# A two-layer decoder trunk: the branch products get PSUM banks of their own, the first merged chunk is split alone, and three steps move later

## The chip, the cores and the metric

The kernel runs on one core of a Trainium2 chip. The metric is the device time of one execution in microseconds (us); lower is better. The engines are called by the names of the profile: PE (TensorE) multiplies matrices, PEld loads its stationary operand, DVE and ACT work element by element, POOL is the fourth engine, and SP issues most of the transfers (DMA).

## The reference

The program computes two layers on x of 256 tokens by 1024 columns, in float32. Cut to what matters here, a layer's first half is:

```python
proj = x @ w_in                      # q, k, v of 8 heads, twice, and two gates of 1024
o_sb = stick_breaking_attention(...) # 256 x 512
o_mb = moba_attention(rope(q_mb), rope(k_mb), v_mb)   # here: causal softmax attention, 256 x 512
merged = sigmoid(g_sb) * (o_sb @ w_branch_sb) + sigmoid(g_moba) * (o_mb @ w_branch_moba)
x = layer_norm(ALPHA * x + merged @ w_out)
```

The second half of a layer is a SwiGLU block with its own normalization, which the change doesn't touch.

## The kernel before, in words

**Arithmetic.** Every float32 operand of a product is held as two parts: `hi`, the value cast to fp32r on ACT, and `lo`, the rest, which DVE subtracts. A product is three matmuls, hi·hi, hi·lo and lo·hi (`mm3`, L433). `split_line` (L349) makes the two parts. Weights come in 122 granules of 128 x 1024 values for each layer. SP loads a granule into one of 6 `raw` buffers, ACT casts it to `whi`, and DVE subtracts to `wlo` (`WeightStream.line`, L159). The next load into a raw buffer waits for the `wlo` of the granule that had it. Both rings hold 10 granules, and `ws.allow` frees a place when PE is done with it.

**Order.** All instructions are recorded by one Python program, in the order in which they will stand on their engines. `Weave` (L35) keeps a planned clock for each engine. Side work is written as generators ("lines") that yield the planned time from which they may go on; while the main program records matmuls, `weave.tick` records every line whose time has come, and `weave.finish` records lines to their end. So a number that is yielded moves instructions on their engines' queues, and every engine works its queue strictly in order.

**PSUM.** There are eight banks, in three pools. `bankM` (L297) gives two tiles of one bank in turn, `bankC` two of one bank, `bankB` two tiles of two banks. An instruction waits for the earlier users of the tile that it writes, and the waits are kept by tile: a matmul into the second bank of a `bankB` tile waits for a DVE read of its first bank.

**Stage by stage.** First come the projections: v and q (`pv`, `pq`), the stick-breaking pairs (`pqk`), k of the second attention (`pk`), its v (`pu`), then eight gate chunks (`pg`, L867), 48 matmuls of 256 columns each. Two heads make a pair, and four pairs of each attention go beside those matmuls. k of the second attention is turned by a round trip through DRAM (`bounce_line`, L511), and `put_kmb` (L884) splits it into `l0kmb_hi` and `l0kmb_lo`. The weights of a pair of the second attention are turned the same way and split into `pp`. Then four matmuls (`l0mb_o`) make the weighted sums of a pair, in two tiles: `bankC` for pairs 0 to 2, `bankM` for pair 3 (`both_parts`, L627). ACT copies one half of each to `f`, DVE adds the rest (four instructions named `l0mb_f`), and `split_line` makes `l0omb_hi` and `l0omb_lo`.

**Around the change.** `branch(i, b, ...)` (L914) multiplies chunk pair i (256 of the 1024 columns) of branch b: 24 matmuls of 256 columns into one bank, over four pairs k of heads. Branch 0 (`l0pa`) needs the first attention and goes while the last pairs of the second one are under way; branch 1 (`l0pb`) needs pair k of the second attention for its k-th part. Before, pa of i = 0 and 1 are the two banks of one `bankB` tile, and so are i = 2 and 3; the same holds for pb. After a branch DVE multiplies its bank with the sigmoid of the gate (`l0gate<-l0gate,l0pa`), for branch 1 it adds the two (`l0gate<-l0gate`), and `split_line` makes the merged chunk pair `l0m_hi`, `l0m_lo`. Branch 1 is recorded as the k = 0, 1 and the k = 2 part of i = 0 to 2, then for each i what is left: 6, 6, 6 and 24 matmuls. Last, `l0pw` multiplies the merged chunks c = 0 to 7 with w_out, for tokens 0 to 127 and then for the rest, in matmuls of 512 columns, six for each chunk; the lo part of a chunk is first used by its third matmul. Layer 1 is the same, with names that begin with l1.

Of the kernel before, what the change touches and what calls it, by code (L numbers as in the profile page):

```python
# [14 lines left out]
P = 128  # L15
DEPTH = 2
D = 1024
S = 256
KC = D // P
DH = 64  # L20
WIDTH = 512
NPAIR = 4
# [12 lines left out]
class Weave:  # L35
# [16 lines left out]
    def dve(self, e, n, f, *args, **kw):  # L52
        f(*args, **kw)  # L53
        self.dve_t = max(self.dve_t, e) + n / 960.0 + DVE_FIXED
        return self.dve_t + HOP
# [195 lines left out]
NSPLIT = 10  # L251
# [9 lines left out]
MARGIN = 0.29  # L261
# [7 lines left out]
def hybrid_trunk_kernel(ctx: ExitStack, tc: tile.TileContext, w, xT_in, x_in, ln_in,  # L269
                        ident_in, mask_in, rope_in, out):  # L270
    nc = tc.nc
# [25 lines left out]
    def bankM(name, shape):  # L297
        return psM.tile(shape, F32, tag="M", name=name)
# [26 lines left out]
    ws = WeightStream(nc, wpool, rings, w, DEPTH * NG_LAYER, weave)  # L325
    act, dve, pool = weave.act, weave.dve, weave.pool
# [72 lines left out]
    hi, lo = (part[:, first[0]] for part in ws.parts[0])  # L399
    e = dve(3.6, 512, nc.vector.tensor_copy, hi, ws.raw[0][:, first[0]])  # L400
# [14 lines left out]
    def late_loads():  # L415
        nc.sync.dma_start(ident, ident_in)
        nc.sync.dma_start(rope, rope_in)
        nc.sync.dma_start(mask, mask_in)
        yield 118.0
        for t in range(2):  # L420
            nc.sync.dma_start(xs[t], x_in[t * P:(t + 1) * P, :])

    weave.add(late_loads(), 12.0)


# [17 lines left out]
    def pe_after(e):  # L443
        weave.t = max(weave.t, e)

    def pe_done():
        return weave.t + HOP
# [80 lines left out]
    def blocked(x):  # L528
        return x.rearrange("p n (i b) -> p n i b", b=32)
# [94 lines left out]
        e = yield from split_line(*parts, pT, 768, e)  # L624
        yield from both_parts(name, p, v, oT, e, p == NPAIR - 1)

    def both_parts(name, p, v, oT, e, in_M=False):  # L627

        turns = []
        if in_M:
            os = [bankM(f"{name}_o{h}", [P, 2, S]) for h in range(2)]
        else:
            for h in range(2):
                turns.append((yield from turn(e)))
            os = [bankC(f"{name}_o{h}", [P, 2, S]) for h in range(2)]
        pe_after(e)
        for h, o in enumerate(os):
            vs = [x[:, p, 2 * h:2 * h + 2, :].rearrange("p r c -> p (r c)") for x in v]  # L640
            mm(o, vs[0], pp[:, :, h, :S], True, False)
            mm(o[:, :, P:], vs[1], pp[:, :, h, S:], False, True)
        e = pe_done()
        summed.append(e)
        yield e
        f = page2.tile([P, S], F32, tag="f", name=f"{name}_f")
        for h, o in enumerate(os):
            e = act(e, S, nc.scalar.copy, f[ROWS[h]], o[ROWS[1 - h], 0, :])
        yield e
        for h, o in enumerate(os):  # L650
            for i in range(2):
                e = dve(e, S, nc.vector.tensor_add, f[ROWS[h]], o[ROWS[h], i, :], f[ROWS[h]])
            if not in_M:
                left[turns[h]] = e
        yield e
        yield from split_line(oT[0][:, p, :], oT[1][:, p, :], f, S, e)
# [150 lines left out]
    for l in range(DEPTH):  # L807
        G = l * NG_LAYER
        L = f"l{l}"
# [18 lines left out]
        else:  # L828
            for t in range(2):
                weave.finish(norms[:t + 1])  # L830
                pe_after(xT_ready[t])
                for j, put in enumerate((put_v, put_q)):
                    ps = bankM(f"{L}pvq{j}{t}", [P, WIDTH])
                    for i in range(4):
                        g = G + 4 * j + i
# [9 lines left out]
        sides, sigmoids, exps, gates, waiting = [], [], [], [], []  # L845
# [36 lines left out]
        k_mb = pair_tiles(L + "kmb", [P, NPAIR, S])  # L882

        def put_kmb(tp, ts, e):  # L884
            return split_line(*(blocked(k[:, :, ts]) for k in k_mb), tp, WIDTH, e)

        both_tokens(f"{L}pk", G + 12, lambda t, ps: ropes.append(weave.start(rope_line(L + "kmb", ps, t, put_kmb))))
        sb_pair(2, G + 16)
# [20 lines left out]
        def rooted():  # L909
            for dst in waiting:  # L910
                act(0.0, 512, nc.scalar.activation, dst, dst, AF.Sigmoid)
            waiting.clear()

        def branch(i, b, ps, ks=range(4)):  # L914
            g = G + 40 + 4 * b + i
            hi, lo = (x.rearrange("p (c k n) -> p c k n", c=2, k=4) for x in ws.take(g))
            o = (o_sb, o_mb)[b]
            for c in range(2):
                for k in ks:
                    mm3(ps[:, c, :], hi[:, c, k, :], lo[:, c, k, :], o[0][:, k, :], o[1][:, k, :],  # L920
                        c == k == 0, c == 1 and k == 3)
            if ks[-1] < 3:
                return 0.0
            ws.allow(g + NSPLIT)
            gated = gates[i][:, :, b, :]
            return dve(pe_done(), 512, nc.vector.tensor_mul, gated, gated, ps)

        if len(exps) == NPAIR:
            rooted()
        for i in range(4):  # L930
            if i % 2 == 0:
                ps = bankB(f"{L}pa{i}", [P, 2, 2, S])
            branch(i, 0, ps[:, i % 2])
        weave.finish(sides[:mb])
        weave.finish(sides[:-2])
        rooted()


        gb = load_gb(l, 0)
        m_t = [pair_tiles(f"{L}m{i}", [P, 4, S]) for i in range(2)]  # L940

        def m_parts(c, n=1):
            return [m[:, c % 4:c % 4 + n, :] if n > 1 else m[:, c % 4, :] for m in m_t[c // 4]]

        pbs = [x for i in range(2) for x in bankB(f"{L}pb{i}", [P, 2, 2, S]).rearrange("p i c n -> i p c n")]
        for ks, upto in ((range(2), -1), (range(2, 3), None)):
            for i in range(3):
                branch(i, 1, pbs[i], ks)
            weave.finish(sides[:upto])
        for i in range(4):  # L950
            e = branch(i, 1, pbs[i], range(3 if i < 3 else 0, 4))
            a, b = (gates[i][:, :, j, :] for j in range(2))
            e = dve(e, 512, nc.vector.tensor_add, a, a, b)
            weave.add(split_line(*m_parts(2 * i, 2), a, 512, e), e)


        norms = []
        for t in range(2):
            acc = bankB(f"{L}pw{t}", [P, 2, 512])
            for c in range(KC):  # L960
                token_out([(512 * h, acc[:, h, :]) for h in range(2)], G + 48 + c, t, *m_parts(c), c == 0, c == KC - 1)
                if t == 1:
                    ws.allow(G + 48 + NSPLIT + c)
            norms.append(weave.start(norm_line(f"{L}a", t, acc, gb)))
# [29 lines left out]
        sides = []  # L994
        for t in range(2):
            weave.finish(norms[:t + 1])
            pe_after(xT_ready[t])
            for j in range(2):
                ps = bankM(f"{L}pft{t}{j}", [P, 512])
                for i in range(4):  # L1000
                    g = G + 56 + 4 * j + i
# [4 lines left out]
        for c in range(NTOK_FC, NFC):  # L1006
            ps = bankM(f"{L}pf{c}", [P, 2, S])
# [12 lines left out]
        g = G + 100  # L1020
# [102 lines left out]
```

## Time and profile before

| | us |
|---|---|
| median of 3 runs (734.68 to 735.06) | 734.88 |
| the profiled execution | 734.4 |
| its span, from the first to the last instruction | 732.5 |
| PE busy, of the span | 712.8 |
| DVE busy | 529.2 |
| ACT busy | 389.1 |
| mean granted clock of TensorE, as a share of full speed | 0.997 |

The profile lists instructions with start and duration in us from the start of the span, the engine, L and the line of the program (helpers have one line: L427 is every matmul, L53 every DVE and L48 every ACT instruction), the operation, and what it writes and reads by the program's names. In brackets stands how long the engine was idle before the instruction and which instruction ended the wait. "x4" is four instructions in a row. Matmuls overlap: one of 256 columns has 0.28 us from start to end, and the next starts 0.11 us after it.

### The profile page before, as it was taken

The numbers are of one execution on the slowest core, as the hardware profiler recorded it, in microseconds if no ns is written. First come the engines' busy times: TensorE is split into PE (matmuls) and PEld (weight loads), VectorE is DVE, ScalarE is ACT, GpSimd is POOL, SyncE is SP. The second block draws the span as 40 slices with busy tenths as digits, with TensorE's granted clock in tenths as the row PEclk, the third lists the DMA queues.
The fourth block names the chain that finished last, engine by engine and source line by source line (L and its number), as shares of the span: only waits on it lengthen the run. The fifth ranks groups of instructions, "written<-read, shape, count | busy, mean of one in ns | idle before, by whom it ended". The sixth has DMA issues, their size and how long they took to land.

```text
span 732.5 us, 12710 instructions
## 1 busy us (share of the span) xinstructions
PE 712.8 (97%) x4984; PEld 652.8 (89%) x4984; DVE 529.2 (72%) x784; ACT 389.1 (53%) x579; POOL 34.5 (5%) x48
## 2 busy tenths in 40 slices
PE   9999999889999999999999999998899999999995
PEld 7989899878899999988889889998788999998885
DVE  5998887688896666644688886868879766665416
ACT  5767667564565554533365566774456545554400
POOL 0001110000000000000000111100010000000001
PEclk9999999999999999999999999999999999999998
DMA  8898889847696656476259678795558965663601
GB/s 301 328 343 222 250 215 268 261 135 238 192 322 227 198 196 198 147 286 200 70 184 342 171 206 232 210 293 193 160 186 263 314 200 199 185 198 104 235 1 58
DMA packets 61597, 156.26 MB, mean 213 GB/s; under 512 B 10721, under 2 KB 21985, under 8 KB 61537
## 3 DMA queue, kind: packets, MB, share of 16 engines
q1 hardware_dynamic: 56848, 140.50, 57.0%
q0 software_dynamic: 4544, 14.68, 9.3%
q8 instruction: 39, 0.64, 0.4%
q10 hardware_dynamic: 144, 0.26, 0.1%
q14 instruction: 22, 0.17, 0.1%
HBM read 148.08 MB, written 7.34 MB: 212 GB/s over the span
## 4 chain that ended last, share of the span: by engine, by line
PE 92%; DVE 4%; DMA 2%; issue 1%; ACT 0%; POOL 0%; DVEq 0%; POOLq 0%; SPq 0%; ACTq 0%
PE l1pf L427 13%; PE l0pf L427 13%; PE l0pd L427 8%; PE l0pg L427 6%; PE l1pg L427 6%; PE l1pe L427 4%; PE l1pd L427 4%; PE l1pft L427 3%; PE l0pw L427 3%; PE l1pqk L427 3%; PE l0pft L427 3%; PE l1pvq L427 3%; PE l1pw L427 3%; PE l0pqk L427 2%; PE l0pv L427 2%; PE l1pk L427 2%
## 5 line engine op out<-in xcount | busy, mean ns | idle before, releaser
L53 DVE TENSOR_TENSOR wlo<-raw,whi 128x1024 fp32r<-128x1024 f32 (+1 forms) x234 | 277.5, 1202 | 82.8 <-ACT whi L48 79.5
L48 ACT CAST whi<-raw 128x1024 fp32r<-128x1024 f32 (+1 forms) x233 | 238.0, 1035 | 84.4 <-PE l0pd L427 19.6
L427 PE MATMUL l1pf<-xT_hi,wlo 128*128 128x256 f32 x288 | 79.6, 276 | 0.0
L427 PE MATMUL l1pf<-xT_hi,whi 128*128 128x256 f32 x288 | 79.6, 276 | 0.0
L427 PE MATMUL l1pf<-xT_lo,whi 128*128 128x256 f32 x288 | 79.6, 276 | 0.0
L427 PE MATMUL l0pf<-xT_hi,wlo 128*128 128x256 f32 x288 | 79.5, 276 | 0.0
L427 PE MATMUL l0pf<-xT_hi,whi 128*128 128x256 f32 x288 | 79.5, 276 | 0.0
L427 PE MATMUL l0pf<-xT_lo,whi 128*128 128x256 f32 x288 | 79.5, 276 | 0.0
L427 PEld LDWEIGHTS l1pf<-xT_hi,whi 128*128 128x128 f32 x288 | 54.1, 188 | 0.0
L427 PEld LDWEIGHTS l1pf<-xT_lo,whi 128*128 128x128 f32 x288 | 54.1, 188 | 0.0
L427 PEld LDWEIGHTS l1pf<-xT_hi,wlo 128*128 128x128 f32 x288 | 54.1, 188 | 0.0
L427 PEld LDWEIGHTS l0pf<-xT_lo,whi 128*128 128x128 f32 x288 | 54.1, 188 | 0.0
L427 PEld LDWEIGHTS l0pf<-xT_hi,whi 128*128 128x128 f32 x288 | 54.1, 188 | 0.0
L427 PEld LDWEIGHTS l0pf<-xT_hi,wlo 128*128 128x128 f32 x288 | 54.1, 188 | 0.0
L427 PE MATMUL l0pg<-xT_hi,whi 128*128 128x256 f32 x128 | 35.8, 280 | 0.8 <-DVE l0vmb L53 0.8
L427 PE MATMUL l1pg<-xT_hi,whi 128*128 128x256 f32 x128 | 35.7, 279 | 0.0
L427 PE MATMUL l0pg<-xT_hi,wlo 128*128 128x256 f32 x128 | 35.4, 277 | 0.0
L427 PE MATMUL l0pg<-xT_lo,whi 128*128 128x256 f32 x128 | 35.4, 277 | 0.0
L427 PE MATMUL l1pg<-xT_hi,wlo 128*128 128x256 f32 x128 | 35.4, 276 | 0.0
L427 PE MATMUL l1pg<-xT_lo,whi 128*128 128x256 f32 x128 | 35.4, 276 | 0.0
L427 PE MATMUL l0pd<-whi,l0h_hi 128*128 128x512 f32 x88 | 34.5, 392 | 0.0
L427 PE MATMUL l0pd<-whi,l0h_lo 128*128 128x512 f32 x88 | 34.3, 389 | 0.0
(349 smaller groups left out, 1784.6 us busy)
## 6 DMA issues: line engine op xcount, KB each, us to landing
raw<-in_w_dram SPq DMA_DIRECT2D x226, 512.0 KB, 4.7
whi<-in_w_dram POOLq DMA_DIRECT2D x14, 512.0 KB, 5.8
wlo<-in_w_dram POOLq DMA_DIRECT2D x14, 512.0 KB, 6.7
ln<-in_ln_dram SPq DMA_DIRECT2D x8, 512.0 KB, 4.2
raw<-in_w_dram SPq DMA_DIRECT2D x7, 256.0 KB, 5.2
l0mb_scr<-l0mb_turn SPq DMA_DIRECT2D x4, 384.0 KB, 4.9
l0mb_turn<-l0mb_scr SPq DMA_DIRECT2D x16, 96.0 KB, 5.3
l1mb_scr<-l1mb_turn SPq DMA_DIRECT2D x4, 384.0 KB, 8.0
```

The source lines that it names most:

```text
L48: f(*args, **kw)
L53: f(*args, **kw)
L427: nc.tensor.matmul(o, a, b, start=start, stop=stop)
```

## The change

- **pa**: each i has a `bankM` tile of one bank, the two tiles in turn, and its gate multiply is recorded right behind its matmuls.
- **pb**: i = 0 and 1 have a `bankM` tile each; i = 2 and 3 share one `bankB` tile, and both of their gate multiplies come after the last matmul of i = 3. The k = 0, 1 part of i = 3 moves ahead of the end of pair 3, so that 12 instead of 24 matmuls are left for it.
- **Last pair**: the weighted sums of pair 3 go to one `bankB` tile, and the line yields `e + MARGIN` ahead of it, so it is recorded later.
- **First chunk**: of the merged pair i = 0 the two chunks are multiplied, added and split one by one, 256 columns each; i = 1 to 3 stay whole. The splits of i = 0 are finished only after the matmuls of i = 3 are recorded, and the others as `l0pw` comes to them.
- **k cast**: `put_kmb` yields `e + 4.0` first.
- **Late loads**: the loads of x are planned at 130 instead of 118, and the scale and shift of the norm (`load_gb`) are recorded after the last pair instead of before it.

```diff
-        yield 118.0
+        yield 130.0
         for t in range(2):
             nc.sync.dma_start(xs[t], x_in[t * P:(t + 1) * P, :])
...
-    def both_parts(name, p, v, oT, e, in_M=False):
+    def both_parts(name, p, v, oT, e, in_B=False):
         turns = []
-        if in_M:
-            os = [bankM(f"{name}_o{h}", [P, 2, S]) for h in range(2)]
+        if in_B:
+            yield e + MARGIN
+            both = bankB(f"{name}_o", [P, 2, 2, S])
+            os = [both[:, h] for h in range(2)]
...
         def put_kmb(tp, ts, e):
-            return split_line(*(blocked(k[:, :, ts]) for k in k_mb), tp, WIDTH, e)
+            yield e + 4.0
+            yield from split_line(*(blocked(k[:, :, ts]) for k in k_mb), tp, WIDTH, e)
...
-            gated = gates[i][:, :, b, :]
-            return dve(pe_done(), 512, nc.vector.tensor_mul, gated, gated, ps)
-        if len(exps) == NPAIR:
-            rooted()
+        def gated(i, b, ps, cs=slice(0, 2)):
+            dst = gates[i][:, cs, b, :]
+            return dve(pe_done(), ps.shape[1] * S, nc.vector.tensor_mul, dst, dst, ps)
+        rooted()
         for i in range(4):
-            if i % 2 == 0:
-                ps = bankB(f"{L}pa{i}", [P, 2, 2, S])
-            branch(i, 0, ps[:, i % 2])
+            ps = bankM(f"{L}pa{i}", [P, 2, S])
+            branch(i, 0, ps)
+            gated(i, 0, ps)
         weave.finish(sides[:mb])
         weave.finish(sides[:-2])
-        rooted()
+        pbs = [bankM(f"{L}pb{i}", [P, 2, S]) for i in range(2)]
+        ps = bankB(f"{L}pb2", [P, 2, 2, S])
+        pbs += [ps[:, 0], ps[:, 1]]
+        for i in range(3):
+            branch(i, 1, pbs[i], range(2))
+        weave.finish(sides[:-1])
+        for i in range(3):
+            branch(i, 1, pbs[i], range(2, 3))
+        branch(3, 1, pbs[3], range(2))
+        weave.finish(sides)
+        pe_after(weave.dve_t)
         gb = load_gb(l, 0)
...
-        pbs = [x for i in range(2) for x in bankB(f"{L}pb{i}", [P, 2, 2, S]).rearrange("p i c n -> i p c n")]
-        for ks, upto in ((range(2), -1), (range(2, 3), None)):
-            for i in range(3):
-                branch(i, 1, pbs[i], ks)
-            weave.finish(sides[:upto])
+        def summed_up(i, c0, n):
+            cs = slice(c0, c0 + n)
+            gated(i, 1, pbs[i][:, cs], cs)
+            a, b = (gates[i][:, cs, j, :] for j in range(2))
+            e = dve(0.0, n * S, nc.vector.tensor_add, a, a, b)
+            hi, lo = (m[:, (2 * i + c0) % 4:(2 * i + c0) % 4 + n, :] for m in m_t[i // 2])
+            side = weave.add(split_line(hi, lo, a, n * S, e), e)
+            m_sides.extend([side] * n)
+        m_sides = []
         for i in range(4):
-            e = branch(i, 1, pbs[i], range(3 if i < 3 else 0, 4))
-            a, b = (gates[i][:, :, j, :] for j in range(2))
-            e = dve(e, 512, nc.vector.tensor_add, a, a, b)
-            weave.add(split_line(*m_parts(2 * i, 2), a, 512, e), e)
+            branch(i, 1, pbs[i], range(3 if i < 3 else 2, 4))
+            for part in (((0, 0, 1), (0, 1, 1)), ((1, 0, 2),), (), ((2, 0, 2), (3, 0, 2)))[i]:
+                if i == 3:
+                    weave.finish(m_sides[:2])
+                summed_up(*part)
...
             for c in range(KC):
+                weave.finish(m_sides[c:c + 1])
                 token_out(...)
```

What this does to the queues shows at three places. The first is PE in layer 0, where the matmuls of pa pass from i = 0 to i = 1. The number behind a name is its buffer, and in brackets stand the engines whose signal the instruction waits for. Before:

```order
L427 MATMUL l0pa_1609<-l0osb_hi,wlo 128x256
L427 MATMUL l0pa_1609<-l0osb_hi,whi 128x256 [waits DVE_49]
L427 MATMUL l0pa_1609<-l0osb_lo,whi 128x256
L427 MATMUL l0pa_1609<-l0osb_hi,wlo 128x256
L427 MATMUL l0pa_1609<-l0osb_hi,whi 128x256
```

And after, at the same place of the queue:

```order
L427 MATMUL l0pa_1607<-l0osb_hi,wlo 128x256
L427 MATMUL l0pa_1644<-l0osb_hi,whi 128x256 [waits Activation_49]
L427 MATMUL l0pa_1644<-l0osb_lo,whi 128x256
L427 MATMUL l0pa_1644<-l0osb_hi,wlo 128x256
L427 MATMUL l0pa_1644<-l0osb_hi,whi 128x256
```

The tile changes there now, and the wait for DVE's gate multiply has become one for ACT, which read the bank's former user, a gate chunk.

The second place is DVE in layer 0 at the end of the branches, from the gate multiply of i = 0 (gate buffers 935, 1131, 1306 and 1455 are i = 0 to 3; `raw` is a weight granule). Before:

```order
L53 TENSOR_TENSOR l0gate_935<-l0gate_935,l0pb_1766 128x2x256
L53 TENSOR_TENSOR l0gate_935<-l0gate_935 128x2x256
L53 TENSOR_TENSOR l0gate_1131<-l0gate_1131,l0pb_1766 128x2x256
L53 TENSOR_TENSOR l0gate_1131<-l0gate_1131 128x2x256
L53 TENSOR_TENSOR l0gate_1306<-l0gate_1306,l0pb_1767 128x2x256
L53 TENSOR_TENSOR l0gate_1306<-l0gate_1306 128x2x256
L53 TENSOR_TENSOR l0m_lo<-l0gate_935,l0m_hi 128x512
L53 TENSOR_TENSOR l0gate_1455<-l0gate_1455,l0pb_1767 128x2x256
L53 TENSOR_TENSOR l0gate_1455<-l0gate_1455 128x2x256
L53 TENSOR_TENSOR wlo<-raw_1666,whi 128x1024
L53 TENSOR_TENSOR l0m_lo<-l0gate_1131,l0m_hi 128x512
```

After, with gate buffers 931, 1129, 1310 and 1455:

```order
L53 TENSOR_TENSOR l0gate_931<-l0gate_931,l0pb_1754 128x256
L53 TENSOR_TENSOR l0gate_931<-l0gate_931 128x256
L53 TENSOR_TENSOR l0gate_931<-l0gate_931,l0pb_1754 128x256
L53 TENSOR_TENSOR l0gate_931<-l0gate_931 128x256
L53 TENSOR_TENSOR l0gate_1129<-l0gate_1129,l0pb_1755 128x2x256
L53 TENSOR_TENSOR l0gate_1129<-l0gate_1129 128x2x256
L53 TENSOR_TENSOR l0m_lo<-l0gate_931,l0m_hi 128x256 x2
L53 TENSOR_TENSOR l0gate_1310<-l0gate_1310,l0pb_1756 128x2x256
L53 TENSOR_TENSOR l0gate_1310<-l0gate_1310 128x2x256
L53 TENSOR_TENSOR l0gate_1455<-l0gate_1455,l0pb_1756 128x2x256
L53 TENSOR_TENSOR l0gate_1455<-l0gate_1455 128x2x256
L53 TENSOR_TENSOR l0m_lo<-l0gate_1129,l0m_hi 128x512
```

The first chunk's four short instructions stand ahead, its lo parts behind the sum of i = 1, and the lo part of i = 1 behind the sums of i = 2 and 3, since those wait for nothing but the last matmul of i = 3. The `wlo` of granule 51 (raw_1666 before), which stood behind the last sum, stands ahead of these rows now.

The third place is DVE in layer 0 where the v of the second attention is split (`l0vmb`, which frees the bank of `l0pu`). Rows with - stand only before, rows with + only after:

```order
 L53 TENSOR_TENSOR l0sb_beta<-l0sb_beta,l0sb_inc 128x2x383
-L53 TENSOR_TENSOR l0kmb_lo<-l0kmb_tok_591,l0kmb_hi 128x4x128
 L53 TENSOR_TENSOR l0vmb_798<-l0pu_800,l0vmb_798 128x4x128
-L53 TENSOR_TENSOR l0kmb_lo<-l0kmb_tok_621,l0kmb_hi 128x4x128
 L53 TENSOR_TENSOR pp<-l0sb_pT,pp 128x768
 L53 TENSOR_TENSOR l0vmb_799<-l0pu_801,l0vmb_799 128x4x128
+L53 TENSOR_TENSOR l0kmb_lo<-l0kmb_tok_591,l0kmb_hi 128x4x128
 L53 TENSOR_TENSOR wlo<-raw_556,whi 128x1024
-L53 TENSOR_TENSOR wlo<-raw_752,whi 128x1024
```

Both splits of k have gone behind both splits of v and the `pp` of a pair of the first attention; ACT's queue changes in the same way.

More of the change, by code (lines that the diff above doesn't have):

```diff
@@ L652, in both_parts @@
                 e = dve(e, S, nc.vector.tensor_add, f[ROWS[h]], o[ROWS[h], i, :], f[ROWS[h]])
-            if not in_M:
+            if not in_B:
                 left[turns[h]] = e
@@ L921, in branch @@
                         c == k == 0, c == 1 and k == 3)
-            if ks[-1] < 3:
-                return 0.0
-            ws.allow(g + NSPLIT)
-            gated = gates[i][:, :, b, :]
-            return dve(pe_done(), 512, nc.vector.tensor_mul, gated, gated, ps)
-        if len(exps) == NPAIR:
-            rooted()
+            if ks[-1] == 3:
+                ws.allow(g + NSPLIT)
+        def gated(i, b, ps, cs=slice(0, 2)):
+            dst = gates[i][:, cs, b, :]
+            return dve(pe_done(), ps.shape[1] * S, nc.vector.tensor_mul, dst, dst, ps)
@@ L939, in hybrid_trunk_kernel @@
+        for i in range(3):
[6 more added lines that the diff above has]
+        pe_after(weave.dve_t)
         gb = load_gb(l, 0)
         m_t = [pair_tiles(f"{L}m{i}", [P, 4, S]) for i in range(2)]
-        def m_parts(c, n=1):
-            return [m[:, c % 4:c % 4 + n, :] if n > 1 else m[:, c % 4, :] for m in m_t[c // 4]]
@@ L945, in hybrid_trunk_kernel, with m_parts @@
-        pbs = [x for i in range(2) for x in bankB(f"{L}pb{i}", [P, 2, 2, S]).rearrange("p i c n -> i p c n")]
-        for ks, upto in ((range(2), -1), (range(2, 3), None)):
-            for i in range(3):
-                branch(i, 1, pbs[i], ks)
-            weave.finish(sides[:upto])
-        for i in range(4):
-            e = branch(i, 1, pbs[i], range(3 if i < 3 else 0, 4))
-            a, b = (gates[i][:, :, j, :] for j in range(2))
-            e = dve(e, 512, nc.vector.tensor_add, a, a, b)
-            weave.add(split_line(*m_parts(2 * i, 2), a, 512, e), e)
+        def m_parts(c):
+            return m_t[c // 4][0][:, c % 4, :], m_t[c // 4][1][:, c % 4, :]
```

## The prediction

> **What bounds the kernel now.** I read the page's engine row and the head of its chain, then what PEld waited for, then the stretches of both layers around the branches.
>
> ```profile
> PE 712.8 (97%) x4984; PEld 652.8 (89%) x4984; DVE 529.2 (72%) x784; ACT 389.1 (53%) x579; POOL 34.5 (5%) x48
> PE 92%; DVE 4%; DMA 2%; issue 1%; ACT 0%; POOL 0%; DVEq 0%; POOLq 0%; SPq 0%; ACTq 0%
> ```
>
> PE is the bound: it holds 92% of the chain that ended last. No matmul is added or removed, so the change can only give or take PE's waits. The waits of PEld (us in total, times, longest) show them better than PE's, because a matmul's end is modelled:
>
> ```profile
> PEld l0pb L427 <- DVE l0gate L53: 2.8, 2, 1.6
> PEld l1pb L427 <- DVE l1gate L53: 2.8, 2, 1.6
> PEld l0pa L427 <- DVE l0gate L53: 2.0, 2, 1.0
> PEld l1pa L427 <- DVE l1gate L53: 2.0, 2, 1.0
> PEld l0pg L427 <- DVE l0vmb L53: 1.2, 1, 1.2
> PEld l0mb_o L427 <- DVE pp L53: 1.0, 1, 1.0
> PEld l1mb_o L427 <- DVE pp L53: 1.0, 1, 1.0
> PEld l0pw L427 <- DVE l0m_lo L53: 0.4, 1, 0.4
> PEld l0pb L427 <- DVE l0omb_lo L53: 0.2, 1, 0.2
> PEld l1pb L427 <- DVE l1omb_lo L53: 0.2, 1, 0.2
> ```
>
> In each layer 2.0 + 1.0 + 2.8 = 5.8 us go at five places of the branch stage, and layer 0 loses 1.2 us at its first gate chunk. With the three small rows the sum is 13.6 us, the most that these edits can give. Now the two branch stages (stretch, sum, then busy PE, PEld, DVE, ACT, POOL, granted clock, DMA share, GB/s):
>
> ```profile
> 130.00:165.00 35.00, 30.12 (x223) 27.51 (x222) 26.78 (x40) 20.95 (x32) 0.00 (x0) 1.00 0.58 195
> 490.00:525.00 35.00, 30.14 (x222) 27.80 (x221) 27.53 (x41) 20.01 (x31) 0.00 (x0) 1.00 0.52 166
> ```
>
> DVE is busy 26.78 of 35 us there. If PE gives up all its waits, DVE has to do nearly the same in some 29 us. So whoever takes PE's waits out meets DVE's queue next.
>
> **The change part by part, on layer 0's clock of the profiled run.** The waits at pa, first on PE, then on DVE:
>
> ```profile
> 132.99 0.28 PE L427 MATMUL l0pa<-l0osb_hi,wlo 128*128 128x256 f32 x1
> 134.12 0.38 PE L427 MATMUL l0pa<-l0osb_hi,whi 128*128 128x256 f32 x1 [0.85 <-DVE l0gate L53]
> ```
> ```profile
> 133.37 0.69 DVE L53 TENSOR_TENSOR l0gate<-l0gate,l0pa 128x512 f32<-128x512 f32 x1 [3.92 <-ACT l0mb_f L48]
> 133.98 1.78 DVE L53 TENSOR_TENSOR l0mb_f<-l0mb_o,l0mb_f 64x256 f32<-64x256 f32 x4
> 135.79 1.23 DVE L53 TENSOR_TENSOR wlo<-raw,whi 128x1024 fp32r<-128x1024 f32 x1
> 137.21 0.69 DVE L53 TENSOR_TENSOR l0gate<-l0gate,l0pa 128x512 f32<-128x512 f32 x1 [0.19 <-PE l0pa L427]
> 137.81 0.95 DVE L53 TENSOR_TENSOR pp<-l0mb_turn,pp 128x768 fp32r<-128x768 f32 x1
> 138.68 0.42 DVE L53 TENSOR_TENSOR l0omb_lo<-l0mb_f,l0omb_hi 128x256 fp32r<-128x256 f32 x1
> ```
> ```profile
> 102.32 22.98 PE l0pg L427 x201
> 125.30 0.70 PE l0mb_o L427 x4
> 163.61 15.54 PE l0pw L427 x67
> ```
>
> The second half of the tile started at 134.12, when the multiply of the first (133.37 + 0.69) was over, though it writes another bank. A matmul of 256 columns takes 22.98 / 201 = 0.114 us, a half of 24 takes 2.74, an `l0pw` matmul 15.54 / 67 = 0.23, the four of a pair 0.70.
>
> *pa in single banks: both waits go.* i = 1 begins at 133.1 and ends at 135.85. i = 2 needs the bank of i = 0, free since 134.06, and ends at 138.6. i = 3 needs the bank of i = 1: its multiply stands behind the sums of pair 1 and a `wlo` (135.79 + 1.23 = 137.02), so the bank is free at 137.7, before 138.6. After 6 matmuls the sums of pair 2 go, 139.3 to 140.0; their `pp` ends some 0.9 behind 137.7, in time.
>
> *Pair 3's wait for its `pp` becomes one for a bank.* The rows of ACT and DVE:
>
> ```profile
> 142.01 0.76 ACT L48 COPY l0mb_f<-l0mb_o 64x256 f32<-64x256 f32 x2 [4.86 <-PE l0mb_o L427]
> 142.79 0.83 ACT L48 CAST pp<-l0mb_turn 128x768 fp32r<-128x768 f32 x1
> 144.23 0.96 DVE L53 TENSOR_TENSOR pp<-l0mb_turn,pp 128x768 fp32r<-128x768 f32 x1
> 145.22 0.69 DVE L53 TENSOR_TENSOR l0gate<-l0gate,l0pa 128x512 f32<-128x512 f32 x1
> ```
>
> DVE takes in turn `l0omb_lo` to 138.9, the multiply of i = 2 to 139.6, a `wlo` to 140.7, pair 2's four additions (1.78) to 142.5, `pp` to 143.4 and the multiply of i = 3 to 144.0. PE ends pa at 140.0 + 18 x 0.114 = 142.05 and the first 12 matmuls of pb at 143.4; the next 12 write the bank that this last multiply reads, and wait 0.7 us. Behind that PE's queue holds all of pb and `l0pw`. The sums of pair 3 follow at 145.45 without a wait, in place of one of 1.0; their `bankB` tile was last used for scores that have long been read.
>
> *pb.* The waits of 2.8 go: i = 0 and 1 have own tiles, and i = 2 and 3 are read only at the end. From 146.15 PE has 12 + 18 + 12 matmuls that need at most pair 2, to 150.9. Pair 3's `l0omb_lo` comes at 151.1 (from 144.0: three `wlo` of some 1.13, `l0omb_lo` of pair 2, pair 3's additions 1.78, another `wlo`, 0.42): 0.2 us of waiting. The 30 matmuls left end at 154.55.
>
> *The first chunk alone.* DVE has a `wlo` first, which ends at 152.2. Two multiplies and two additions of 256 columns (0.42, by the `l0omb_lo` row, with no cover for a result that is read at once) take to 153.9, the pair i = 1 to 155.25, and the first lo part is there at 155.65. `l0pw` begins at 154.55, and its third matmul, due at 155.0, waits 0.7. Chunk 2's third is due at 158.45; its lo part stands behind four instructions of i = 2 and 3 (2.65 us) and ends at 159.2: 0.8 us more. Later chunks have two `wlo` ahead of them and come in time.
>
> Split instructions cost more. Two of 256 cost 2 x 0.42 where one of 512 costs 0.69: three on DVE are split, so 0.45 us of DVE is added, and it lies in chunk 2's wait, already counted. ACT's cast is split too, where ACT waits for DVE anyway. The rows say that the first lo part would come at 155.9 unsplit, so that the split gains 0.25 at chunk 0 and loses 0.45 at chunk 2. [...]
>
> New waits: 0.7 + 0.2 + 0.7 + 0.8 = 2.4 us a layer. In layer 1 the queue differs by an exchange of `pp` and a multiply, and I take the same. No row shows these waits. They are no less than 0, if DVE gets ahead, and no more than 3.6 if one more `wlo` (1.23) stands ahead of a multiply; 2.4 follows from the rows.
>
> *k cast later.*
>
> ```profile
> 78.12 0.68 DVE L53 TENSOR_TENSOR l0kmb_lo<-l0kmb_tok,l0kmb_hi 128x512 fp32r<-128x512 f32 x1
> 78.72 0.68 DVE L53 TENSOR_TENSOR l0vmb<-l0pu,l0vmb 128x512 fp32r<-128x512 f32 x1
> 79.46 0.38 PE L427 MATMUL l0pg<-xT_hi,whi 128*128 128x256 f32 x1 [0.78 <-DVE l0vmb L53]
> 90.42 1.57 PE l0mb_s L559 x21
> ```
>
> `l0vmb` moves up by 78.72 - 78.12 = 0.6 us, and so does PE; the other 0.6 of the 1.2 stays, since DVE's earlier work ends at 78.1. The second split of k, then at about 83, must be there for the scores (`l0mb_s`) at 90.42, which move up by 12 matmuls and the 0.6: 5 us of cover, and if that were gone, the delay in full. Layer 1 has no such wait in the rows: nothing.
>
> *Late loads.*
>
> ```profile
> 131.00 0.91 SPq L421 DMA_DIRECT2D x<-in_x_dram  x2
> 137.05 5.06 SPq L137 DMA_DIRECT2D raw<-in_w_dram  x2
> 142.16 2.51 SPq L801 DMA_DIRECT2D ln<-in_ln_dram  x2
> 171.65 0.69 DVE L53 SCALAR_TENSOR_TENSOR x<-x,l0pw 128x512 f32<-128x512 f32 x1
> 174.51 0.75 DVE L53 SCALAR_TENSOR_TENSOR x<-x,l0a_nmu,ln 128x512 f32<-128x512 f32 x1 [1.31 <-ACT l0pw L48]
> ```
>
> x goes behind two weight loads, `ln` behind four more. They are read at 171.65 and 174.51, 20 us later: nothing, and the weights get the ring sooner.
>
> **Sum.** Layer 0: 5.8 + 0.4 + 0.2 - 2.4 = 4.0, and 0.6 at the k cast. Layer 1: 5.8 + 0.2 - 2.4 = 3.6. Together 8.2 us: the profiled 734.4 (a span of 732.5 and 1.9 around it) becomes 726.2. The median, 734.88, lies 0.5 above that execution, so I forecast 726.7.
>
> **The rivals.**
>
> *All waits go* (DVE gets ahead of PE everywhere): up to 13.6 - 0.6 = 13.0 us, 721.9. For it: DVE sits idle 3.92 us ahead of 133.37. Against it: DVE's chain from 138.7 on is work back to back.
>
> *DVE takes most of it back*: each layer's new waits double to 4.8, because 26.78 us of work hardly fits; the gain is 3.4, 731.5. For it: all five waits of a stage before were for DVE. Against it: DVE's idle ahead of 133.37, which PE's wait did not cause.
>
> *No change*: the second bank still waits, by the chip and not by the tile. Against it: at 134.12 PE followed the end of a named instruction by 0.06 us, and that wait is no longer in its queue. 734.9.
>
> *Slower*: the load of granule 51. Its `wlo` moves from behind the last sum to ahead of the first chunk's multiply, and DVE's queue stands still if the load is late. The load is issued at 137.05, and ACT comes to its cast behind that of pair 3's sums, at about 150.1, 13 us later. The loads of `raw` land after (least, median, most):
>
> ```profile
> DMA to landing us min/median/max: 2.7/4.7/9.1
> ```
>
> It costs nothing up to 13 us, and the kernel is slower than before only from 13 + 4.1 = 17 us in both layers. At 19 us it would be 734.88 - 8.2 + 2 x 6 = 738.7. The longest load argues against it.
>
> **How the numbers follow.** The forecast's case 0.80 (gains of 5 to 11 us), all waits go 0.07, most taken back 0.07, no change 0.03, slower 0.03. The low end is half of the new waits, 8.2 + 2.4 = 10.6, 724.3. The high end is 3.6 in each layer and nothing at the k cast, 8.2 - 2.4 - 0.6 = 5.2, 729.7; that leaves out 2 in 10. About 0.2% (1.5 us) is what a measurement can tell from no change. Faster 0.94, same 0.03, slower 0.03.
>
> **What would show it.** Right: no PEld wait for a gate multiply within pa; one of 0.7 us at pb's second tile, for DVE; none at `l0mb_o`; `l0pw` waiting 0.7 and 0.8 us for `l0m_lo` at chunks 0 and 2; 0.6 us left at `l0pg`. Wrong: waits at pa that stay, a wait for `raw` or `whi` in the branch stage, or `l0mb_s` waiting for `l0kmb_lo`.

## The result, and the profile after

The changed kernel takes 725.98 us (median of 4 runs, 725.66 to 726.24), and the kernel before took 734.78 on the same chip. The ratio is 0.9881 (95% interval 0.9864 to 0.9898): 8.8 us faster, where 8.2 were forecast (726.7). The profiled span falls from 732.5 to 724.2.

The engine row and the head of the chain of the page after:

```profile
PE 711.6 (98%) x4984; PEld 652.0 (90%) x4984; DVE 528.8 (73%) x790; ACT 389.8 (54%) x581; POOL 34.5 (5%) x48
PE 84%; DVE 8%; DMA 4%; issue 2%; ACT 1%; POOL 0%; SPq 0%; DVEq 0%; POOLq 0%; ACTq 0%
```

PE has as many matmuls as before and nearly the same busy time, in a shorter span. DVE has six instructions more, three a layer, and a larger part of the chain. What PEld waited for at the places of the prediction:

```profile
PEld l0pw L427 <- DVE l0m_lo L53: 2.2, 3, 1.0
PEld l1pw L427 <- DVE l1m_lo L53: 1.8, 2, 1.0
PEld l0pb L427 <- DVE l0gate L53: 0.8, 1, 0.8
PEld l0pg L427 <- DVE l0vmb L53: 0.6, 1, 0.6
PEld l1pb L427 <- DVE l1gate L53: 0.6, 1, 0.6
PEld l1pb L427 <- DVE l1omb_lo L53: 0.3, 1, 0.3
```

There is no row for `pa` and none for `mb_o` any more, and the 3.0 us of `pb` in each layer (gates and `omb_lo`) have become 0.8 and 0.9. `pw`, which had 0.4 in layer 0 alone, now has 2.2 and 1.8. The two branch stages, in the columns of before:

```profile
130.00:165.00 35.00, 33.37 (x239) 30.41 (x238) 31.38 (x48) 22.12 (x34) 0.00 (x0) 1.00 0.70 231
490.00:525.00 35.00, 33.56 (x218) 29.66 (x217) 32.70 (x50) 18.78 (x28) 0.00 (x0) 1.00 0.67 212
```

DVE went from 26.78 to 31.38 of 35 us in layer 0: the stretch holds 48 of its instructions in place of 40, since the stage is done sooner.

What PE itself loses is read from starts. Between two matmuls of 256 columns lie 0.114 us, between two of 512 columns 0.23; what is over is lost. PE of layer 0, the three places in order of time, and then the four of layer 1:

```profile
142.87 0.28 PE L427 MATMUL l0pb<-l0omb_hi,wlo 128*128 128x256 f32 x1
143.75 0.38 PE L427 MATMUL l0pb<-l0omb_hi,whi 128*128 128x256 f32 x1 [0.60 <-DVE l0gate L53]
...
154.40 0.40 PE L427 MATMUL l0pw<-wlo,l0m_hi 128*128 128x512 f32 x1
155.27 0.50 PE L427 MATMUL l0pw<-whi,l0m_lo 128*128 128x512 f32 x1 [0.47 <-DVE l0m_lo L53]
155.60 0.39 PE L427 MATMUL l0pw<-whi,l0m_hi 128*128 128x512 f32 x1
...
157.90 0.39 PE L427 MATMUL l0pw<-wlo,l0m_hi 128*128 128x512 f32 x1
158.85 0.50 PE L427 MATMUL l0pw<-whi,l0m_lo 128*128 128x512 f32 x1 [0.56 <-DVE l0m_lo L53]
```
```profile
497.91 0.28 PE L427 MATMUL l1pb<-l1omb_hi,wlo 128*128 128x256 f32 x1
498.56 0.39 PE L427 MATMUL l1pb<-l1omb_hi,whi 128*128 128x256 f32 x1 [0.38 <-DVE l1gate L53]
...
505.56 0.28 PE L427 MATMUL l1pb<-l1omb_hi,whi 128*128 128x256 f32 x1
505.94 0.39 PE L427 MATMUL l1pb<-l1omb_lo,whi 128*128 128x256 f32 x1
...
509.61 0.40 PE L427 MATMUL l1pw<-wlo,l1m_hi 128*128 128x512 f32 x1
510.44 0.50 PE L427 MATMUL l1pw<-whi,l1m_lo 128*128 128x512 f32 x1 [0.43 <-DVE l1m_lo L53]
...
513.10 0.39 PE L427 MATMUL l1pw<-wlo,l1m_hi 128*128 128x512 f32 x1
514.02 0.50 PE L427 MATMUL l1pw<-whi,l1m_lo 128*128 128x512 f32 x1 [0.53 <-DVE l1m_lo L53]
```

Layer 0 loses 0.77, 0.64 and 0.72 us, layer 1 loses 0.54, 0.27, 0.60 and 0.69: 2.1 us in each. Every such stop costs a little more behind it: the next matmul starts 0.11 us later than it otherwise would (0.33 from 155.27 to 155.60, where 0.23 is usual). DVE between the first and the second of these places in layer 0:

```profile
143.01 0.69 DVE L53 TENSOR_TENSOR l0gate<-l0gate,l0pa 128x512 f32<-128x512 f32 x1
143.61 2.35 DVE L53 TENSOR_TENSOR wlo<-raw,whi 128x1024 fp32r<-128x1024 f32 x2
145.88 0.42 DVE L53 TENSOR_TENSOR l0omb_lo<-l0mb_f,l0omb_hi 128x256 fp32r<-128x256 f32 x1
146.22 1.22 DVE L53 TENSOR_TENSOR wlo<-raw,whi 128x1024 fp32r<-128x1024 f32 x1
147.35 1.76 DVE L53 TENSOR_TENSOR l0mb_f<-l0mb_o,l0mb_f 64x256 f32<-64x256 f32 x4
149.15 1.23 DVE L53 TENSOR_TENSOR wlo<-raw,whi 128x1024 fp32r<-128x1024 f32 x1
150.29 0.42 DVE L53 TENSOR_TENSOR l0omb_lo<-l0mb_f,l0omb_hi 128x256 fp32r<-128x256 f32 x1
150.63 1.22 DVE L53 TENSOR_TENSOR wlo<-raw,whi 128x1024 fp32r<-128x1024 f32 x1
151.88 0.42 DVE L53 TENSOR_TENSOR l0gate<-l0gate,l0pb 128x256 f32<-128x256 f32 x1
```

No row has a bracket: from the last gate multiply of branch 0 on, DVE works back to back in layer 0. In layer 1 there is one hole, ahead of pair 3's additions:

```profile
501.38 1.77 DVE L53 TENSOR_TENSOR l1mb_f<-l1mb_o,l1mb_f 64x256 f32<-64x256 f32 x4 [0.27 <-ACT l1mb_f L48]
```

The additions start 1.48 us after the `wlo` ahead of them, where 1.13 is usual (146.22 to 147.35 in layer 0). So DVE loses some 0.34 us there, and several of the runs below close this hole.

**A finer measure.** The spans of profiles differ by more than some edits are worth, but nearly all of that lies at the start: from the start to the first `l0pqk` matmul the profiles of this study take 27.1 to 28.8 us, whatever the kernel. Behind it, equal stretches repeat within a few hundredths, with two exceptions at the k cast that are told below. So three stretches of PE are read from the timeline: from the first `l0pu` matmul to the first `l0pg` ("k cast"), and in each layer from the first matmul of pa to the first of `pft`, the first product behind `pw` ("stage").

| kernel | time, us | k cast | stage, layer 0 | stage, layer 1 |
|---|---|---|---|---|
| before | 734.78 | 14.38 | 53.69 | 53.31 |
| after | 725.98 | 13.78 | 49.48 | 49.63 |
| after, once more | 725.92 | 13.78 | 49.49 | 49.65 |
| pa shared | 729.06 | 13.77 | 51.23 | 50.91 |
| k cast early | 726.34 | 14.37 | 49.49 | 49.29 |
| loads early | 725.58 | 14.21 | 49.46 | 49.68 |
| first pair whole | 725.23 | 13.77 | 48.99 | 49.33 |
| order 0, 2, 1 | 725.66 | 13.78 | 49.46 | 49.30 |
| pb in double banks | 728.66 | 13.78 | 51.79 | 50.01 |
| pa alone | 731.18 | 14.38 | 51.85 | 51.54 |
| additions on POOL | 725.27 | 13.78 | 49.61 | 49.37 |
| more DVE work | 728.99 | 13.78 | 50.79 | 50.63 |
| lo in turn | 725.15 | 14.36 | 49.26 | 48.81 |
| lo in turn, chunk 4 first | 724.20 | 13.78 | 48.29 | 48.79 |

The gain is 4.21 + 3.68 in the stages and 0.60 at the k cast, 8.49 in all.

### The profile page after: what moved, and what is told of

The parts are those of the page before. It is cut to its first block, busy times and chain, and to the rows that moved or that the text cites. A ratio compares the mean times of both kernels' runs of the same rounds, so it can differ in the third digit from the quotient of the medians.

```text
span 724.2 us, 12718 instructions
## 1 busy us (share of the span) xinstructions
PE 711.6 (98%) x4984; PEld 652.0 (90%) x4984; DVE 528.8 (73%) x790; ACT 389.8 (54%) x581; POOL 34.5 (5%) x48
## 4 chain that ended last, share of the span: by engine, by line
PE 84%; DVE 8%; DMA 4%; issue 2%; ACT 1%; POOL 0%; SPq 0%; DVEq 0%; POOLq 0%; ACTq 0%
PE l1pf L427 14%; PE l0pf L427 14%; PE l0pd L427 8%; PE l0pg L427 6%; PE l1pe L427 4%; PE l1pd L427 4%; PE l1pqk L427 3%; PE l0pqk L427 3%; PE l1pvq L427 3%; PE l0pft L427 3%; DVE wlo L53 3%; PE l0pw L427 3%; PE l1pg L427 2%; DMA l1mb_scr<-l1mb_turn 2%; PE l1pw L427 2%; PE l0pv L427 2%
```

## The experiments

The profile already speaks against the prediction's rivals, so the question is what the time now hangs on. **Queue theory:** from the last gate multiply of branch 0 on, DVE's queue bounds the stage. A wait of PE costs only as far as it delays that queue, or as PE is still late behind it; what is taken out at one place comes back at the next. **Every wait in full:** each wait of PE is a loss by itself, and goes or comes with its edit. Third, the **late loads** could have given the time by easing DMA.

**pa shared again.**

```diff
-            ps = bankM(f"{L}pa{i}", [P, 2, S])
-            branch(i, 0, ps)
-            gated(i, 0, ps)
+            if i % 2 == 0:
+                ps = bankB(f"{L}pa{i}", [P, 2, 2, S])
+            branch(i, 0, ps[:, i % 2])
+            gated(i, 0, ps[:, i % 2])
```

> The changed kernel with one edit undone: pa of i = 0 and 1, and of i = 2 and 3, are again two banks of one tile; every queue keeps its order. Theory (DVE's queue bounds the branch stage from pair 2's additions on, so that a wait of PE counts only as far as it delays that queue): PE waits 1.0 us twice at pa, pair 2's additions come 1.5 us later instead of 2.0, since DVE's weight split stands ahead of them anyway, and the later wait for the bank of i = 3 shrinks by as much: 1.5 us a layer, 726.0 + 3.0 = 729.0. Rival (each wait that went counts in full): 2.0 us a layer, 730.0. Rival (the gain came from the later loads): 726.0.

Measured 729.06, ratio to before 0.9927 (0.9913 to 0.9940). What PEld waited for in it:

```profile
PEld l0pa L427 <- DVE l0gate L53: 2.0, 2, 1.0
PEld l1pa L427 <- DVE l1gate L53: 2.0, 2, 1.0
```

4.0 us of waits are back, and there is no row any more for the gate at pb's second tile: PE now comes there later. The stages grow by 1.75 + 1.28 = 3.03. The loads stand where the change puts them, and 3.1 of the 8.8 us are lost all the same. That is the 3.0 of the queue theory; its rival had 4.0.

**k cast early.** The line `yield e + 4.0` is taken out.

> The changed kernel without the delay of k's cast. Both theories: PE's wait at the first gate chunk of layer 0 goes from 0.6 back to 1.2 us, nothing in layer 1: 726.6. Rival (the later cast moved more than that, through the sums of the last stick-breaking pairs): over 727.5.

Measured 726.34, ratio 0.9890 (0.9877 to 0.9904). The time can't tell 0.4 us, but the stretch does: 14.37 instead of 13.78. (In layer 1 the planner put a `wlo` ahead of the additions of pair 3 instead of behind them, in this kernel as in the one with the order 0, 2, 1. That fills the hole in DVE's queue, and both stages there are some 0.34 shorter.)

**Loads early.** x is planned at 118 again, and `load_gb` recorded ahead of branch 1:

```diff
-        yield 130.0
+        yield 118.0
...
+        gb = load_gb(l, 0)
         pbs = [bankM(f"{L}pb{i}", [P, 2, S]) for i in range(2)]
```

> The changed kernel with the loads of x planned at 118 again and the norm's scale and shift recorded ahead of the last pair; the queues of PE and DVE stay as they are. Theory: 726.0, nothing, since both are read 20 us later and no weight is waited for in the branch stage. Rival (transfers were what made the stage slow): 728 or more, with waits for raw or whi in the branch stage.

Measured 725.58, ratio 0.9882 (0.9869 to 0.9896), with the same stages. The late loads are worth nothing, and that theory falls.

**First pair whole.** The two chunks of i = 0 go together, as those of i = 1 to 3 do.

```diff
-            for part in (((0, 0, 1), (0, 1, 1)), ((1, 0, 2),), (), ((2, 0, 2), (3, 0, 2)))[i]:
+            for part in (((0, 0, 2),), ((1, 0, 2),), (), ((2, 0, 2), (3, 0, 2)))[i]:
```

> The changed kernel with the first merged pair multiplied, added and split whole. Theory: the first lo part comes 0.2 us later and the one of i = 1 some 0.4 earlier; l0pw waits 0.85 and 0.4 instead of 0.63 and 0.72: -0.1 us a layer, 725.8. Rival (the fixed cost of the short instructions counts in full): -0.45 us a layer, 725.1. Rival (the split is worth what chunk 0 would wait without it): 726.5 or more.

Measured 725.23, ratio 0.9873 (0.9860 to 0.9887). Chunk 0 and chunk 2 of layer 0 in it:

```profile
153.87 0.40 PE L427 MATMUL l0pw<-wlo,l0m_hi 128*128 128x512 f32 x1
154.73 0.50 PE L427 MATMUL l0pw<-whi,l0m_lo 128*128 128x512 f32 x1 [0.47 <-DVE l0m_lo L53]
...
157.38 0.40 PE L427 MATMUL l0pw<-wlo,l0m_hi 128*128 128x512 f32 x1
157.98 0.50 PE L427 MATMUL l0pw<-whi,l0m_lo 128*128 128x512 f32 x1 [0.20 <-DVE l0m_lo L53]
```

Chunk 0 loses 0.63 as before, chunk 2 only 0.37 in place of 0.72. So the split brings its first lo part no earlier and costs 0.35 us at chunk 2; by the stages 0.49 and 0.30, 0.8 us in both layers. Its part of the change is a loss, nearer to the rival's 0.45 a layer than to the 0.1 that I had expected.

**Order 0, 2, 1.** The wait at pb's second tile is taken away by an order in which that bank is written 12 matmuls later.

```diff
-        for i in range(3):
+        for i in (0, 2, 1):
             branch(i, 1, pbs[i], range(2))
```

> The halves of branch 1 go in the order i = 0, 2, 1, so the bank of i = 1, which the last gate multiply of branch 0 still reads, is written 12 matmuls later: the wait of 0.76 us (layer 0) and 0.54 us (layer 1) at pb's second tile goes. DVE's instructions stay as they are. If DVE's queue is what bounds the stage, l0pw's waits for m_lo grow by what this wait gives, and the time stays: 726.0 (725.5 to 726.4). If every PE wait counts in full: 726.0 - 1.3 = 724.7.

Measured 725.66, ratio 0.9883 (0.9870 to 0.9896). This is the sharpest test. PEld in it:

```profile
PEld l0pw L427 <- DVE l0m_lo L53: 2.1, 3, 1.0
PEld l1pw L427 <- DVE l1m_lo L53: 1.9, 2, 1.0
...
PEld l0pb L427 <- DVE l0omb_lo L53: 0.8, 1, 0.8
...
PEld l1pb L427 <- DVE l1omb_lo L53: 0.6, 1, 0.6
```

The 0.8 and 0.6 us are there in the same size, now for `omb_lo`, the next thing that PE needs of DVE, and `pw` waits as before. (In layer 1 the 0.3 for `omb_lo` of before is part of the 0.6, and DVE's order differs, as said; the test is layer 0.) Layer 0, whose DVE queue is unchanged, takes 49.46 instead of 49.48. I had expected the wait at `pw`; it came back one step earlier. For every wait in full 0.77 us should have gone there.

**pb in double banks.** Branch 1 gets two `bankB` tiles, and pair 3 the two `bankM` ones; the order of DVE's work stays the changed one.

```diff
-            both = bankB(f"{name}_o", [P, 2, 2, S])
-            os = [both[:, h] for h in range(2)]
+            os = [bankM(f"{name}_o{h}", [P, 2, S]) for h in range(2)]
...
-        pbs = [bankM(f"{L}pb{i}", [P, 2, S]) for i in range(2)]
-        ps = bankB(f"{L}pb2", [P, 2, 2, S])
-        pbs += [ps[:, 0], ps[:, 1]]
+        pbs = []
+        for i in range(2):
+            ps = bankB(f"{L}pb{i}", [P, 2, 2, S])
+            pbs += [ps[:, 0], ps[:, 1]]
```

> The halves of branch 1 lie in two double-bank tiles as before the change, and pair 3's weighted sum in the two single banks; the gate multiplies and their place at the end are the change's. The last 6 matmuls of i = 1 must then wait for both multiplies of i = 0 (about 1.3 us a layer), and the wait of 0.76/0.54 at pb's second tile goes. Queue theory: DVE is late only by some 0.35 us a layer, since it stands for that time at an addition of i = 0 and then waits for i = 1: 726.7. Every wait in full: + 1.3 x 2 - 1.3 = 727.3. If single banks for branch 1 were most of what the change gives there, it would come out at 731 or more.

Measured 728.66, ratio 0.9920 (0.9904 to 0.9935), but its 6 runs spread from 726.48 to 731.48, and in its profile the granted clock was 0.95 in the stretch from 130 to 165 us of layer 0. Layer 1, at a granted clock of 1.00, takes 50.01, 0.38 more than after. There PE waits 1.7 us for the gate multiply and `pw` only 0.7:

```profile
PEld l1pb L427 <- DVE l1gate L53: 1.7, 1, 1.7
...
PEld l1pw L427 <- DVE l1m_lo L53: 0.7, 1, 0.7
```

So a new wait of 1.7 us costs 0.4 net, and two things make up that sum. DVE stands idle for the last matmuls of i = 1 (0.59 us ahead of 510.62, some 0.7 from start to start). But the gate wait of 0.54 earlier in the stage is gone, pair 3's sums come sooner, and the hole of 0.34 in DVE's queue is closed. The queue theory expected 0.35 without that hole, so it is luck that the size agrees. Of the 1.9 us that layer 1 gains beyond pa (51.54 with pa alone, below, to 49.63) the banks of branch 1 and pair 3 give 0.4. The other 1.5 are left, by subtraction, for the rest of the change, of which the split of the first chunk is a loss of 0.3; I put them down to the new order of matmuls and multiplies in branch 1, but no run has that order alone. The time itself decides nothing here.

**pa alone.** The kernel before, with branch 0 in four `bankM` tiles and nothing else.

> The kernel before with branch 0's halves in four single-bank tiles and nothing else of the change. The four waits of 1.0 us for a gate multiply inside pa go. If every wait counts in full: 734.8 - 4.0 = 730.8. Queue theory: DVE's additions, pp and last gate multiply stay nearly where they were on PE's clock, part of the time comes back at mb_o and at pb's second tile: gain 3.3, 731.5. If single banks work only together with the new order of branch 1: 734 to 735.

Measured 731.18, ratio 0.9953 (0.9941 to 0.9964): 3.4 us faster than before, 3.6 by the stages. That lies between 3.3 and 4.0 and doesn't tell the two apart. It does show that this part works without the others, and what becomes of its gain:

```profile
PEld l0mb_o L427 <- issue: 1.5, 1, 1.5
...
PEld l0mb_o L427 <- DVE l0gate L53: 0.4, 1, 0.4
```

By PEld's rows `mb_o` waits 1.9 us where it waited 1.0. (`issue` stands where the profile shows no releaser; PE's own row of that wait names DVE's `pp`.)

**Additions on POOL.** The first pair whole, and the additions of i = 2 and 3 given to POOL, so that 1.4 us leave DVE's queue ahead of chunk 2.

```diff
-            e = dve(0.0, n * S, nc.vector.tensor_add, a, a, b)
+            if i < 2:
+                e = dve(0.0, n * S, nc.vector.tensor_add, a, a, b)
+            else:
+                e = pool(weave.dve_t + HOP, nc.gpsimd.tensor_tensor, a, a, b, op=OP.add)
```

> The first chunk isn't split alone (as in the run with the whole first pair), and the additions of i = 2 and 3 go to POOL: 2 x 0.69 us leave DVE's queue ahead of m_lo of i = 1. Queue theory: chunk 2's wait (0.37 and 0.38 us in the run without POOL) goes, chunk 0's (0.64 and 0.61) stays: 725.2 - 0.75 = 724.5. If DVE isn't what that wait hangs on: 725.2. If POOL's addition takes over 3 us each, the later chunks wait for it: 726 or more.

Measured 725.27, ratio 0.9872 (0.9858 to 0.9887): nothing gained on 725.23. Chunk 2's wait did go, but chunk 4 of layer 0 now waits 1.2 us. DVE and POOL in layer 0:

```profile
157.34 1.48 DVE L53 TENSOR_TENSOR l0m_lo<-l0gate,l0m_hi 128x512 fp32r<-128x512 f32 x1
158.74 3.45 DVE L53 TENSOR_TENSOR wlo<-raw,whi 128x1024 fp32r<-128x1024 f32 x2
```
```profile
156.98 3.00 POOL L58 TENSOR_TENSOR l0gate<-l0gate 128x512 f32<-128x512 f32 x2 [40.40 <-DVE l0gate L53]
```

While POOL adds, an `m_lo` takes 1.48 us (0.68 elsewhere), and two `wlo` 3.45 (2.35). DVE loses 1.9 us to save 1.4. The wait hung on DVE, as the theory has it; its forecast of the time failed on a cost that no trace had shown.

**More DVE work, and the change once more.** Two instructions that change no value are put behind the last gate multiply of branch 0:

```diff
+        for i in range(2):
+            both = gates[3][:, :, 1, :]
+            dve(0.0, 512, nc.vector.tensor_max, both, both, both)
```

> The changed kernel itself once more, beside the three runs below on one chip: 726.0 by every theory, so that their differences to it can be read directly.

> Behind the last gate multiply of branch 0, DVE takes the maximum of half a gate tile with itself, twice (128x512, 0.61 us of queue each; the values stay the same): 1.2 us of DVE work a layer that nobody waits for. Queue theory: from there to m_lo DVE has no idle time, so PE loses nearly all of it, at omb_lo and then at the first chunks: + 2.2 to 2.6 us, 728.4. If DVE still has room (it is idle 3.6 of the 35 us of the stretch) the time stays at 726.0.

Measured 725.92 (ratio 0.9880, 0.9867 to 0.9894) and 728.99 (0.9925, 0.9911 to 0.9938). The two instructions take 1.41 us, and the stages grow by 1.31 and 0.99 (2.3 by the stages, 3.1 by the medians). Where PE lost them:

```profile
PEld l1pb L427 <- DVE l1omb_lo L53: 1.3, 1, 1.3
```

The wait at `omb_lo` of layer 1 goes from 0.3 to 1.3, and `pw` waits as before. From start to start the two instructions hold DVE's queue for 1.33 us. Layer 0 loses nearly all of it; in layer 1 the hole of 0.34 ahead of pair 3's additions is closed, and 1.33 - 0.34 = 0.99 is lost. DVE's idle time elsewhere in the stretch is no room for work at this place.

**Lo in turn.** If the place in DVE's queue decides, the lo parts should stand where PE needs them. Both kernels have the first pair whole, and `m_lo` of i = 0 and 1 move ahead of the next addition; the second also finishes `m_lo` of i = 2 before chunk 3's matmuls.

```diff
+                gated(j, 1, pbs[j])
+                if 0 < j < 3:
+                    weave.finish(m_sides[2 * j - 2:2 * j])
+                summed_up(j)
...
                 weave.finish(m_sides[c:c + 1])
+                if c == 3:
+                    weave.finish(m_sides[4:6])
```

> The first chunk isn't split alone, and m_lo of i = 0 goes ahead of the addition of i = 1, m_lo of i = 1 ahead of the addition of i = 2. DVE's work is that of the run with the whole first pair (725.2), only its order differs. Queue theory, by place in the queue: l0pw's and l1pw's waits for chunks 0 and 2 (1.0 us a layer there) go in both layers. In layer 0 a second wlo now stands ahead of m_lo of i = 2, which ends 1.1 us after chunk 4 needs it, so that layer gives all of it back; in layer 1 one wlo stands there and nothing is late: 724.3. Every wait in full: 723.2. If the amount of DVE's work bounds the stage, whatever its order: 725.2.

> As the run before it, and m_lo of i = 2 is put ahead of the second wlo in layer 0 (it is issued before chunk 3's matmuls). Queue theory: chunk 4 no longer waits, m_lo of i = 3 and the wlo of chunk 6 come just in time (0 to 0.3 us late): 723.3. If the amount of DVE's work bounds the stage, whatever its order: 725.2.

Measured 725.15 (ratio 0.9871, 0.9857 to 0.9884) and 724.20 (0.9859, 0.9846 to 0.9873). In the first, chunk 4 of layer 0 waits as forecast:

```profile
160.95 0.39 PE L427 MATMUL l0pw<-wlo,l0m_hi 128*128 128x512 f32 x1
162.36 0.50 PE L427 MATMUL l0pw<-whi,l0m_lo 128*128 128x512 f32 x1 [1.03 <-DVE l0m_lo L53]
```

1.41 - 0.23 = 1.2 us, and layer 0 gives everything back and 0.27 more (49.26 against 48.99). Layer 1 gains 0.52, where 1.0 was expected. In the second, `pw` waits for its lo parts in small pieces:

```profile
PEld l0pw L427 <- DVE l0m_lo L53: 0.9, 3, 0.3
...
PEld l1pw L427 <- DVE l1m_lo L53: 0.7, 2, 0.4
...
PEld l1pw L427 <- DVE wlo L53: 0.5, 1, 0.5
```

Layer 0 gains 0.70 and layer 1 0.54 on the first pair whole, 1.2 us where 1.9 were forecast: the direction is shown, and the size was too large. The trace shows much of the rest: `pw` still stops three times in each layer, every stop costs its 0.11 us behind it, and in layer 1 one of them is a new one, 0.2 us by PE's starts, for a `wlo`. That the amount of DVE's work alone bounds the stage is refuted. This kernel has the shortest time of the study, 1.7 us below the change on the same chip (725.92), 2.1 by the stages.

## Why the prediction was right, step by step

- **PE bounds, and only its waits can be won.** Right: the gain is found in the three stretches that were named, and to 0.2 us nowhere else behind the start.
- **The waits of 5.8 us a layer go.** Right: none of the five waits is left.
- **New waits of 2.4 us a layer** (0.7 at pb's second tile, 0.2 for `omb_lo` of pair 3, 0.7 at chunk 0, 0.8 at chunk 2). Measured 0.77, too little for a row, 0.64 and 0.72 in layer 0, and 0.54, 0.27, 0.60 and 0.69 in layer 1: 2.1 in each. The four places and who is waited for are as forecast. The term was 0.3 us a layer too large by these gaps. Another was left out: the start that comes 0.11 us late behind every stop. Counted with it, the waits fall from 6.7 to 2.6 us in layer 0 (5.8 + 0.4 + 0.2 to 2.4 in the sum) and from 6.4 to 2.8 in layer 1 (5.8 + 0.2 to 2.4). That is 4.1 and 3.6, where the sum had 4.0 and 3.6 and the stages gave 4.21 and 3.68. So the sum is as good as that partly by luck: what it left out on both sides nearly cancels. The forecast of the time missed by 0.7. At the profiled run it was 0.2 (726.2 against 725.96); the other 0.5 is how far the median of before lay above its profiled run, and after the two are the same.
- **Layer 1 like layer 0.** Right within 0.2 us, though the waits are shared out differently.
- **The first chunk alone** was the mis-sized step. It was to gain 0.25 at chunk 0 and lose 0.45 at chunk 2. It gains nothing at chunk 0 and loses 0.35 at chunk 2. The 0.25 doesn't follow from the prediction's own rows: unsplit, 152.2 + 4 x 0.69 + 0.69 is 155.65, the very time that it gives for the split, and not 155.9. The first lo part stands behind the whole pair i = 1 either way, and the two more instructions ahead of it (0.26 us by the runs, 2.91 against 2.65 from the first multiply to the first `m_lo`) take what the shorter `m_lo` saves (0.42 against 0.68). The price of splitting was right by the rows: 0.42 us for 256 columns, 0.69 for 512, so two halves take an estimated 2 x 0.42 - 0.69 = 0.15 us longer than a whole. That price was a better guide here than the gain that the prediction saw.
- **k cast.** Right: 14.38 to 13.78, the 0.6 forecast. `l0kmb_lo` of the second half starts at 82.26 and its reader at 88.76, so the 5 us of cover are there:

```profile
82.26 0.69 DVE L53 TENSOR_TENSOR l0kmb_lo<-l0kmb_tok,l0kmb_hi 128x512 fp32r<-128x512 f32 x1
```

  It isn't firm, though: in two of the eleven profiles with the late cast (loads early, lo in turn) the stretch took 14.21 and 14.36. Some 6 us earlier DVE had waited 0.71 and 0.86 us for ACT's `l0sb_keep` there, and 0.28 in the run of after; the differences, 0.43 and 0.58, are those of the stretches. So DVE's earlier work does set what is left of this wait, as the prediction said. Why ACT was later there wasn't tried.
- **Late loads: nothing.** Shown by the run with the early loads.
- **The rivals.** *All waits go*: four places still wait. *DVE takes most of it back*: it takes 2.1 of 5.8 us, and more DVE work shows how near this was, since 1.33 us more of DVE's queue there cost PE 1.31 and 0.99. *No change*: the waits inside pa went with the tiles, and came back with them. *Slower by granule 51*: its `wlo` at 150.63 stands in the row above without a bracket, so its load was in time.

What the prediction didn't say is how its terms hang together. It added waits as if each were a loss by itself, and that came out because the new waits of the whole chain were worked out with it. Undoing one part shows the difference: pa's 4.0 us of waits cost 3.0, and pb's wait of 1.7 us cost 0.4 net.

## What to carry to other kernels

Where a wait is taken out, follow the queue of the engine that was waited for to the next thing that is needed of it: if that queue has no idle time, the wait moves there in its full size, as the 0.77 us at pb's second tile of layer 0 came back as 0.78 at `omb_lo` (a hole in the queue takes up its part, as the 0.34 us of layer 1 did), and only work taken from the queue, or put behind what is needed first, gains anything. Splitting an instruction to get a first half early pays only if the half doesn't stand behind other work in the queue anyway; here it brought nothing at chunk 0 and cost 0.35 us at chunk 2. And when edits are worth less than the scatter of whole runs, compare stretches between two fixed instructions in the traces.

## What the runs showed of the hardware

- POOL and DVE took longer side by side, in the run with the additions on POOL. Two additions of 128x512 on POOL took 3.00 us and ended at 159.98; the two `wlo` that DVE had begun in between ended at 162.19, 2.21 later, about their full length of 2.35. POOL's first addition was over by 158.30, when ACT's cast read its sum, at most 1.32 us after its start; the second, begun beside DVE's `m_lo` (1.48 us, 0.68 elsewhere), ended no less than 1.68 after that. Of the two multiplies of the gates ahead of that `m_lo`, which read one operand from PSUM, the second still ran when POOL began; together they took 1.28 us, as two `m_lo` did at 162.11, after POOL was done.
- DVE worked in the order in which the program recorded its instructions. After the change, in layer 0, ACT had the hi part of the pair i = 1 at 155.53 (154.91 + 0.62), and its `l0m_lo` started at 158.11, behind the sums of i = 2 and 3, the last of which started at 157.50.
- An instruction of DVE that read the result of the one ahead of it started 0.46 us after that one for 256 columns (151.88 to 152.34 in layer 0 after the change) and 0.71 for 512 (153.47 to 154.18); one that read nothing of it started 0.34 and 0.61 after it (152.34 to 152.68, 154.18 to 154.79).
- A stop of PE costs more than the gap that shows: the next matmul starts 0.11 us late as well, for 256 columns (0.22 us behind the one that waited, where 0.11 is usual) as for 512 (0.33, where 0.23 is usual).
- The time from the start to the first `l0pqk` matmul varied from 27.1 to 28.8 us between profiles, while the stretches behind it repeated within 0.03 us (49.48 and 49.49, 49.63 and 49.65 for the same kernel).
